# A fused transformer block: where the first block's scores, values and gate are worked out, by which engine and in which step

## The chip, the cores and the metric

The kernel runs on one core of one Trainium2 chip. Its metric is the time of one execution on the device in microseconds. The kernel before was timed three times: 1420.10, 1420.78 and 1422.68 us, median 1420.78 us. One further execution was recorded by the hardware profiler; it took 1421.69 us, and all rows below are from it.

The engines are named as the profile names them: TensorE (PE; PEld is its weight load), VectorE (DVE), ScalarE (ACT), GpSimd (POOL) and SyncE (SP).

## What is computed

A token row of 512 positions, with 16 meta tokens ahead of it (528 keys), passes a forgetting-attention mixer, a SwiGLU, a gated linear recurrence and a second feed-forward network. The change lies in the first of these alone:

```python
def fox_mixer(h, w_in, b_f, q_gain, k_gain, w_out):
    proj = h @ w_in
    q, k, v, gate, f_logit = jnp.split(proj, [D, 2 * D, 3 * D, 4 * D], axis=-1)
    q = rms_norm(q.reshape(B, L, FOX_HEADS, FOX_HEAD_DIM), q_gain)
    k = rms_norm(k.reshape(B, L, FOX_HEADS, FOX_HEAD_DIM), k_gain)
    log_f = jax.nn.log_sigmoid(f_logit + b_f)
    c = jnp.cumsum(log_f, axis=1).transpose(0, 2, 1)
    ...
    s = jnp.einsum('bhqd,bhkd->bhqk', q_blk, k) * (FOX_HEAD_DIM ** -0.5)
    s = s + (c_q[..., :, None] - c_k[..., None, :])
    s = jnp.where(pos_k[None, :] <= pos_q[:, None], s, -jnp.inf)
    p = jax.nn.softmax(s, axis=-1)
    o = jnp.einsum('bhqk,bhkd->bhqd', p, v)
    ...
    o = o * jax.nn.sigmoid(gate)
    return o @ w_out
```

There are 16 heads of 64 channels (D is 1024) and four blocks of 128 queries; block i sees 16 + 128 (i + 1) keys, so 144, 272, 400 and 528.

## The kernel before, in words

**Tiling and staging.** Two heads make a pair that fills 128 partitions; there are eight pairs, t = 0 to 7. For each pair the four projections q, k, v and gate are made one after the other. Products are taken in a high and a low part of each operand, which makes three matmuls for each of the eight 128-row tiles of the contraction. q and gate have one PSUM tile of 512 columns, k and v two of 264. ScalarE writes the high part of the next weights (L170), VectorE the low part (L180).

**The order of the work.** The loop at the end of `fox` advances a `Weave` once per eighth of a projection: one step is three matmuls of 512 columns or six of 264, and a pair has 32 steps (q is steps 0 to 7, k 8 to 15, v 16 to 23, gate 24 to 31). What else a pair needs is entered in the weave with `at(delay, fn)`, so that it is issued between the matmuls of a later step; every engine then runs its instructions in the order in which they were issued. The delays stand in one row of constants (`F_V` to `F_0`), with special tuples for the first pairs (`K_0`, `Q_1`). A step called 10' below is step 10 of the pair whose projections are being made; the attention work in it is that of the pair before.

**What is woven in.** `head_norm` takes a finished q or k out of PSUM (L392), squares it on ScalarE (L394) and, as high and low part, on GpSimd (L396, L397), sums the squares per head on TensorE into a tile `tp` (L323), and forms the inverse root by L222, L225 and L226 on ScalarE and L224, L229 and L230 on VectorE; L406 scales q or k by it. `got_g` takes the gate out, forms a log-sigmoid (L467, L468 and L472 on ScalarE, L473 and L474 on GpSimd) and its exponential (L477).

`attend` has eight units u = 2 i + s for query block i and head s. `scores` makes the logits in PSUM (L502 the mask, L504 and L506 the products), the row maximum (L510, L512) and the exponential with its row sum (L515). For u = 6 and 7 the 528 keys do not fit one tile and make two pieces of 264. Two steps later `scaled` multiplies the probabilities by the inverse sum (L521, L523). Eight steps after its scores, `flip` transposes the unit on TensorE (L535) into one or two tiles and copies them out: L537 on ScalarE or L539 on VectorE, as the table `F_E` says for each unit. `values` multiplies the flipped probabilities of both heads with v into the tile `plog` (L547), and `gated` multiplies that with the gate (L553).

**PSUM tiles.** `mm` has three tiles, which q, the two of k, the two of v and the gate take in turn; so the second tile of v is the first of k, and has to be read out by L392 before v's matmuls may write it. `tp` has two: the sums, the flips, the flip of v (L422) and the second score pieces all take them in turn. `py` has two, for the scores; `plog` has one.

**Steps.** For the pairs t = 2 to 7, u0 to u4 are scored at the end of the pair's own steps and in 0' to 5', u6 at 7', u7 at 9', flips at two-step distance up to 17', values at 9', 13', 17' and 21', `gated` at 23'. The sums of q are issued at 10', those of k at 18'.

Of the kernel before, what the change touches and what calls it, by code (L numbers as in the profile page):

```python
# [20 lines left out]
F32 = mybir.dt.float32  # L21
# [4 lines left out]
AF = mybir.ActivationFunctionType  # L26
OP = mybir.AluOpType
# [3 lines left out]
P = 128  # L31
D = 1024
KT = D // P
T = 512
# [35 lines left out]

A_W, A_Q, A_K, A_R = 1, 1, 2, 5

F_E = 1, 1, 1, 1, 1, 0, 0, 0


F_V, Q_U, Q_R, Q_H, Q_L, K_U, K_R, K_H, K_L, F_S, F_F, F_O, F_G, F_N, F_0 = 6, 3, 2, 12, 1, 2, 2, 6, 2, 12, 8, 4, 12, 2, 5

K_0, Q_1 = (7, 2, 10, 2), (5, 2, 12, 1)


class Weave:
# [5 lines left out]
    def at(self, delay, fn, *args):  # L87
        self.todo.setdefault(self.step + delay, []).append((fn, args))
# [11 lines left out]
class Net:  # L100
# [147 lines left out]
    def fox(self):  # L248
        nc, tc, a = self.nc, self.tc, self.a
# [8 lines left out]
        pp = self.pp  # L258

        def mm():  # L260
            return pp.tile([P, T], F32, name="mm", bufs=3)
# [23 lines left out]
        NB = T // P  # L285
# [62 lines left out]
        def f_bank():  # L348
            return pp.tile([P, T], F32, name="py", bufs=2)
# [34 lines left out]
        at = w.at  # L384
# [28 lines left out]
        def got_v(t, pv):  # L413
            v1 = wk.tile([P, TM], F32, name="v1", bufs=1)
            for p, o, n in pv:
                nc.vector.tensor_mul(v1[:, o:o + n], p, r1[:, o:o + n])

            def flip():
                vt = vts[t % 2]
                tp = pp.tile([P, T], F32, name="tp", bufs=2)  # L420
                for j in range(NB):
                    nc.tensor.transpose(tp[:, j * P:(j + 1) * P], v1[:, j * P:(j + 1) * P], self.ident)  # L422
                nc.scalar.activation(vt[:, 0:NB].rearrange("p j d -> p (j d)"), tp, AF.Copy)
                tp = pp.tile([P, T], F32, name="tp", bufs=2)
                nc.tensor.transpose(tp[:NM, :P], v1[:, T:TM], self.ident)
                nc.vector.tensor_copy(vt[:NM, NB], tp[:NM, :P])

            at(F_V, flip)

        def got_q(t, pq):  # L430

# [28 lines left out]
        def got_g(t, pg):  # L460
            sg = wk.tile([P, T], F32, name="sg", bufs=2)
            nc.vector.tensor_mul(sg, pg[0][0], r1[:, NM:])


            def exponential():
                e = sgs[t, 1] = wk.tile([P, T], F32, name="se", bufs=1)
                nc.scalar.activation(e, sg, AF.Abs)  # L467
                nc.scalar.activation(e, e, AF.Exp, scale=-1.0)  # L468

            def logarithm():  # L470
                e = sgs[t, 1]
                nc.scalar.activation(e, e, AF.Ln, bias=1.0)  # L472
                nc.gpsimd.tensor_scalar(sg, sg, 0.0, None, op0=OP.min)  # L473
                nc.gpsimd.tensor_sub(sg, sg, e)  # L474

            def sigmoid():
                nc.scalar.activation(sg, sg, AF.Exp)  # L477

            at(F_G, exponential)
            at(F_G + 2, logarithm)  # L480
            at(F_G + 6, sigmoid)
            sgs[t] = sg
# [3 lines left out]
        def attend(t):  # L486
            vt = vts[t % 2]
            pts, po = [], []

            def scores(i, s):  # L490
                kw = NM + P * (i + 1)
                qi = slice(i * P, (i + 1) * P)
                ps = pp.tile([P, T], F32, name="py", bufs=2)
                if kw > T:
                    n = kw // 2
                    pieces = [(ps, 0, n), (pp.tile([P, T], F32, name="tp", bufs=2), n, n)]
                else:
                    pieces = [(ps, 0, kw)]
                for p, o, n in pieces:
                    m0 = max(o, kw - P)  # L500
                    if m0 < o + n:
                        nc.tensor.matmul(p[:, m0 - o:n], self.identb, self.maskb, start=True, stop=False,  # L502
                                         skip_group_check=True)
                    nc.tensor.matmul(p[:, :n], qs[:, s, qi], kd[:, s, o:o + n], start=(m0 >= o + n), stop=False,  # L504
                                     skip_group_check=True)
                    nc.tensor.matmul(p[:, :n], q2[:, s, qi], k2[:, s, o:o + n], start=False, stop=True,  # L506
                                     skip_group_check=True)
                mx = wk.tile([P, 6], F32, name="mx", bufs=4)
                for e, (p, o, n) in enumerate(pieces):
                    nc.vector.tensor_reduce(mx[:, e:e + 1], p[:, :n], axis=AX.X, op=OP.max, negate=True)  # L510
                if len(pieces) > 1:
                    nc.vector.tensor_tensor(mx[:, 0:1], mx[:, 0:1], mx[:, 1:2], op=OP.min)  # L512
                for e, (p, o, n) in enumerate(pieces):
                    c = pt_off[i] + o
                    nc.scalar.activation(pb[s][:, c:c + n], p[:, :n], AF.Exp, bias=mx[:, 0:1],  # L515
                                         accum_out=mx[:, 2 + e:3 + e])

                def scaled():
                    if len(pieces) > 1:
                        nc.vector.tensor_add(mx[:, 2:3], mx[:, 2:3], mx[:, 3:4])  # L520
                    nc.vector.reciprocal(mx[:, 4:5], mx[:, 2:3])  # L521
                    pbi = pb[s][:, pt_off[i]:pt_off[i] + kw]
                    nc.vector.tensor_scalar(pbi, pbi, mx[:, 4:5], None, op0=OP.mult)  # L523

                at(F_N, scaled)

            def flip(i, s):
                if i == 0:
                    pts.append(wk.tile([P, PW], F32, name=f"pt{s}", bufs=1))
                for j0 in range(0, i + 2, 4):  # L530
                    n = min(4, i + 2 - j0) * P
                    c = pt_off[i] + j0 * P
                    tp = pp.tile([P, T], F32, name="tp", bufs=2)
                    for o in range(0, n, P):
                        nc.tensor.transpose(tp[:, o:o + P], pb[s][:, c + o:c + o + P], self.ident)  # L535
                    if F_E[2 * i + s]:
                        nc.scalar.activation(pts[s][:, c:c + n], tp[:, :n], AF.Copy)  # L537
                    else:
                        nc.vector.tensor_copy(pts[s][:, c:c + n], tp[:, :n])  # L539

            def values(i):
                if i == 0:
                    po.append(pp.tile([P, T], F32, name="plog", bufs=1))
                for j in range(i + 2):
                    c = pt_off[i] + j * P
                    for s in range(2):
                        nc.tensor.matmul(po[0][s * HD:(s + 1) * HD, i * P:(i + 1) * P],  # L547
                                         vt[:, j, s * HD:(s + 1) * HD], pts[s][:, c:c + P],
                                         start=(j == 0), stop=(j == i + 1), skip_group_check=True)

            def gated():
                sg = sgs[t]
                nc.vector.tensor_mul(sg, po[0], sg)  # L553
                nc.scalar.activation(ogh[:, t], sg, AF.Copy)

            def gated_lo():
                sg = sgs.pop(t)
                nc.vector.tensor_sub(ogl[:, t], sg, ogh[:, t].bitcast(F32))

            s0 = F_S + (0 if t else F_0)  # L560
            for u in range(2 * NB):
                at(s0 + 2 * u, scores, u // 2, u % 2)
                at(s0 + F_F + 2 * u, flip, u // 2, u % 2)
            for i in range(NB):
                at(s0 + F_F + F_O + 4 * i + 2, values, i)
            at(s0 + F_F + F_O + 4 * NB, gated)
            at(s0 + F_F + F_O + 4 * NB + 2, gated_lo)

        kinds = ((got_q, False), (got_k, True), (got_v, True), (got_g, False))
        forget_1()  # L570
        got_q(0, q0)
# [15 lines left out]
        for n in range(self.EARLY):  # L587
            p = mm() if n < 3 else f_bank()
# [16 lines left out]
        for m in range(KT):  # L605
            if m < self.EARLY:
                p = early[m]
            else:
                p = mm()
# [1037 lines left out]
```

## Time and profile before

| | |
|---|---|
| median of three runs | 1420.78 us |
| profiled execution | 1421.69 us |
| its span | 1419.9 us |
| TensorE busy | 1349.7 us, 95% |
| VectorE busy | 741.5 us, 52% |
| ScalarE busy | 535.6 us, 38% |
| GpSimd busy | 143.9 us, 10% |

The span reaches from the first to the last instruction; 1.79 us of the execution lie outside it. The first block's attention lies between about 40 and 340 us of the span, and repeats every 37 us. Shares of busy time are means over the whole kernel, most of which the change does not touch, so the rows below are from the attention alone. [...]

### The profile page before, as it was taken

The numbers are of one execution on the slowest core, as the hardware profiler recorded it, in microseconds if no ns is written. First come the engines' busy times: TensorE is split into PE (matmuls) and PEld (weight loads), VectorE is DVE, ScalarE is ACT, GpSimd is POOL, SyncE is SP. The second block draws the span as 40 slices with busy tenths as digits, with TensorE's granted clock in tenths as the row PEclk, the third lists the DMA queues.
The fourth block names the chain that finished last, engine by engine and source line by source line (L and its number), as shares of the span: only waits on it lengthen the run. The fifth ranks groups of instructions, "written<-read, shape, count | busy, mean of one in ns | idle before, by whom it ended". The sixth has DMA issues, their size and how long they took to land.

```text
span 1419.9 us, 20806 instructions
## 1 busy us (share of the span) xinstructions
PE 1349.7 (95%) x8506; PEld 1027.8 (72%) x8506; DVE 741.5 (52%) x1321; ACT 535.6 (38%) x988; POOL 143.9 (10%) x127
## 2 busy tenths in 40 slices
PE   7899999999999999999999999999999999988895
PEld 6788888888788888888887888875656656545452
DVE  7887788784654433444455666533342342332234
ACT  6766666664523222323443354522111111111114
POOL 2312222211200000000322121000000000000001
PEclk9999999999999999999999999999999999999998
DMA  4111111113332322223221222698999999999994
GB/s 161 69 44 61 60 61 60 60 60 119 116 111 90 109 99 89 89 94 113 90 89 60 89 90 81 263 400 322 404 421 419 420 420 421 420 419 421 420 421 195
DMA packets 41346, 282.26 MB, mean 199 GB/s; under 512 B 4736, under 2 KB 4992, under 8 KB 7840
## 3 DMA queue, kind: packets, MB, share of 16 engines
q1 hardware_dynamic: 40464, 280.05, 49.6%
q8 instruction: 68, 1.11, 0.3%
q10 hardware_dynamic: 784, 0.85, 0.2%
q14 instruction: 30, 0.25, 0.1%
HBM read 278.72 MB, written 2.10 MB: 198 GB/s over the span
## 4 chain that ended last, share of the span: by engine, by line
PE 70%; DMA 13%; DVE 9%; ACT 4%; issue 1%; POOL 1%; SPq 0%; ACTq 0%; DVEq 0%; POOLq 0%
PE mm L207 20%; PE mm L336 8%; PE py L207 8%; PE tp L207 8%; DMA wring<-in_w_dram 7%; PE tp L1269 5%; PE plog L1322 4%; DMA v<-in_w_dram 3%; DMA wraw<-in_w_dram 3%; PE py L1301 3%; PE mm L792 2%; PE tp L1280 1%; DVE pb L523 1%; PE mm L1287 1%; PE plog L547 1%
## 5 line engine op out<-in xcount | busy, mean ns | idle before, releaser
L180 DVE TENSOR_TENSOR whl<-wraw,whl 128x1024 fp32r<-128x1024 f32 x138 | 181.5, 1315 | 102.4 <-ACT whl L170 102.1
L336 PE MATMUL mm<-xh,whl 128*128 128x264 f32 (+1 forms) x736 | 183.5, 333 | 3.8 <-DVE q L392 2.8
L170 ACT ACTIVATE whl<-wraw 128x1024 fp32r<-128x1024 f32 x138 | 144.5, 1050 | 109.6 <-PE mm L207 45.9
L207 PE MATMUL mm<-xh,whl 128*128 128x512 f32 x544 | 176.1, 397 | 0.0
L336 PEld LDWEIGHTS mm<-xh,whl 128*128 128x128 f32 x736 | 120.8, 191 | 18.8 <-issue 3.4
L1269 PEld LDWEIGHTS tp<-h,xt 128*128 128x128 f32 x992 | 114.2, 194 | 19.1 <-PE plog L1322 7.5
L1269 PE MATMUL tp<-h,xt 128*128 128x128 f32 x992 | 120.1, 280 | 0.0
L207 PEld LDWEIGHTS mm<-xh,whl 128*128 128x128 f32 x544 | 102.3, 188 | 23.0 <-issue 2.3
L207 PE MATMUL mm<-xl,whl 128*128 128x512 f32 x272 | 106.2, 390 | 0.0
L1282 DVE COPY sv<-tp 128x3 f32<-128x3 f32 x16 | 2.6, 160 | 188.2 <-PE tp L1280 188.2
L336 PE MATMUL mm<-xl,whl 128*128 128x264 f32 (+1 forms) x368 | 100.0, 325 | 0.0
L1272 ACT ACTIVATE h<-tp,vecs 128x128 f32<-128x128 f32 x124 | 35.3, 368 | 158.1 <-PE tp L1269 158.1
L1322 PE MATMUL plog<-wring,h 128*32 128x512 f32 x624 | 72.8, 596 | 8.6 <-ACT h L1272 4.6
L1289 DVE TENSOR_TENSOR acc<-acc,mm 128x512 f32<-128x512 f32 (+1 forms) x120 | 73.2, 673 | 6.0 <-PE mm L1288 6.0
L207 PE MATMUL mm<-ogh,whl 128*128 128x512 f32 x224 | 73.8, 396 | 0.0
L635 POOL TENSOR_TENSOR ss<-ss,sq 128x512 f32<-128x512 f32 x21 | 29.1, 1401 | 371.1 <-ACT sq L631 349.1
L207 PE MATMUL py<-xh,whl 128*128 128x512 f32 x208 | 65.9, 392 | 0.0
L207 PE MATMUL tp<-xh,whl 128*128 128x512 f32 x208 | 65.2, 390 | 0.0
L336 PEld LDWEIGHTS mm<-xl,whl 128*128 128x128 f32 x368 | 62.2, 191 | 3.0
L207 PEld LDWEIGHTS mm<-xl,whl 128*128 128x128 f32 x272 | 51.2, 188 | 11.5 <-issue 1.4
L1287 PE MATMUL mm<-h,ss 128*128 128x512 f32 (+1 forms) x128 | 56.5, 442 | 2.2 <-DVE acc L1289 0.5
L1451 POOL TENSOR_TENSOR wring<-acc,wring 128x512 f32<-128x512 f32 x4 | 5.0, 1282 | 494.6 <-DVE acc L1289 494.6
(438 smaller groups left out, 2508.5 us busy)
## 6 DMA issues: line engine op xcount, KB each, us to landing
wring<-in_w_dram SPq DMA_DIRECT2D x124, 1024.0 KB, 19.8
wraw<-in_wd_dram SPq DMA_DIRECT2D x69, 1024.0 KB, 4.7
whl<-in_w_dram SPq DMA_DIRECT2D x27, 1024.0 KB, 19.8
v<-in_w_dram SPq DMA_DIRECT2D x20, 1024.0 KB, 19.8
wraw<-in_w_dram SPq DMA_DIRECT2D x18, 1024.0 KB, 19.8
h<-in_xT_dram SPq DMA_DIRECT2D x8, 256.0 KB, 6.1
acc<-in_w_dram SPq DMA_DIRECT2D x2, 1024.0 KB
out_dram<-wring SPq DMA_DIRECT2D x4, 512.0 KB, 4.7
```

The lines of the kernel that those rows point to most:

```text
L170: self.nc.scalar.activation(hl[:, 0], raw, AF.Copy)
L180: self.nc.vector.tensor_sub(hl[:, 1], raw, hl[:, 0].bitcast(F32))
L207: self.nc.tensor.matmul(out, w, x[:, first + k], start=(at + k == 0 and e == 0), stop=(at + k == of - 1 and e == 2))
L336: nc.tensor.matmul(p[:rows, :m], w[:, wi, k], xx[:, k, o:o + m], start=(n == 0), stop=(n == 3 * KT - 1))
L635: nc.gpsimd.tensor_add(ss, ss, sq)
L792: nc.tensor.matmul(pv[b], x[:, k, bs], w2[:, wi, k % 2], start=(k == 0 and e == 0), stop=(k == KT - 1 and e == 2))
L1269: nc.tensor.matmul(p[:, k], self.xt[:, b, (k0 + k) * P:(k0 + k + 1) * P], oh[:, 1, b], start=(b + k == 0), stop=(b == NB - 1), skip_group_ ...
L1272: nc.scalar.activation(xs[:, k0 + k], p[:, k], AF.Copy, scale=self.vec(V_FN2, k0 + k))
L1287: nc.tensor.matmul(pc, gt[:, b * P:(b + 1) * P], yh[:, hs], start=True, stop=False)
L1289: nc.vector.tensor_add(acc[b][:, hs], acc[b][:, hs] if q else self.xt[:, b, hs], pc)
L1301: nc.tensor.matmul(py[js, o:o + c], hT[:, e, js], w, start=(e == 0), stop=(e == 1), skip_group_check=True)
L1322: nc.tensor.matmul(ps[32 * j:32 * j + 32], xs[:, k, 32 * j:32 * j + 32], self.ring[q, k][:, j * T:(j + 1) * T], start=(k == 0), stop=(k == ...
```

## The change

The second score piece of u = 6 and 7 goes to the tile `plog` and no longer to `tp`, its exponential is issued ahead of that of the first piece, and u7 is scored and flipped one step later (10' and 18'). The values are taken four steps later (`F_O` 8 for 4), so at 13', 17', 21' and 25', and `gated` at 27'. The multiplication by the inverse sum goes from VectorE to ScalarE. The two GpSimd steps of the gate become one VectorE instruction. The flip of u7 is copied out by ScalarE (the last entry of `F_E`), the sums of k are issued a step later (`K_U`, 3 for 2), those of q for pair 1 two steps earlier (`Q_1`), and the flip of v of pair 0 three steps later (`V_0`).

```diff
-F_E = 1, 1, 1, 1, 1, 0, 0, 0
+F_E = 1, 1, 1, 1, 1, 0, 0, 1
...
-F_V, Q_U, Q_R, Q_H, Q_L, K_U, K_R, K_H, K_L, F_S, F_F, F_O, F_G, F_N, F_0 = 6, 3, 2, 12, 1, 2, 2, 6, 2, 12, 8, 4, 12, 2, 5
+F_V, Q_U, Q_R, Q_H, Q_L, K_U, K_R, K_H, K_L, F_S, F_F, F_O, F_G, F_N, F_0 = 6, 3, 2, 12, 1, 3, 2, 6, 2, 12, 8, 8, 12, 2, 5
-K_0, Q_1 = (7, 2, 10, 2), (5, 2, 12, 1)
+K_0, Q_1, V_0 = (7, 2, 10, 2), (3, 2, 14, 1), 9
...
-            at(F_V, flip)
+            at(F_V if t else V_0, flip)
...
-                nc.gpsimd.tensor_scalar(sg, sg, 0.0, None, op0=OP.min)
-                nc.gpsimd.tensor_sub(sg, sg, e)
+                nc.vector.scalar_tensor_tensor(sg, sg, 0.0, e, op0=OP.min, op1=OP.subtract)
...
-                    pieces = [(ps, 0, n), (pp.tile([P, T], F32, name="tp", bufs=2), n, n)]
+                    pieces = [(ps, 0, n), (pp.tile([P, T], F32, name="plog", bufs=1), n, n)]
...
-                for e, (p, o, n) in enumerate(pieces):
+                for e, (p, o, n) in reversed(list(enumerate(pieces))):
...
-                    nc.vector.tensor_scalar(pbi, pbi, mx[:, 4:5], None, op0=OP.mult)
+                    nc.scalar.activation(pbi, pbi, AF.Copy, scale=mx[:, 4:5])
...
             for u in range(2 * NB):
-                at(s0 + 2 * u, scores, u // 2, u % 2)
-                at(s0 + F_F + 2 * u, flip, u // 2, u % 2)
+                last = int(u + 1 == 2 * NB)
+                at(s0 + 2 * u + last, scores, u // 2, u % 2)
+                at(s0 + F_F + 2 * u + last, flip, u // 2, u % 2)
```

The line numbers of the changed kernel are those of the kernel before up to L472; in it the new VectorE instruction is L473, the exponential of the gate L476, and the multiplication, now on ScalarE, keeps L523.

**ScalarE, pair in the steady state, from u6's exponentials to the inverse root of q.** Before (`pb_128` and `pb_129` hold the probabilities of the two heads, `pt_` the flipped ones, `rr` is the root's tile):

```order
L515 ACTIVATE pb_128,mx<-py,mx 128x264
L515 ACTIVATE pb_128,mx<-tp,mx 128x264
L170 ACTIVATE whl<-wraw 128x1024
L537 ACTIVATE pt_2253<-tp 128x384
L515 ACTIVATE pb_129,mx<-py,mx 128x264
L515 ACTIVATE pb_129,mx<-tp,mx 128x264
L222 ACTIVATE rr<-tp,epsc 128x512
```

And in the changed kernel:

```order
L515 ACTIVATE pb_128,mx<-plog,mx 128x264
L515 ACTIVATE pb_128,mx<-py,mx 128x264
L523 ACTIVATE pb_129<-pb_129,mx 128x400
L170 ACTIVATE whl<-wraw 128x1024
L537 ACTIVATE pt_2249<-tp 128x384
L523 ACTIVATE pb_128<-pb_128,mx 128x528
L515 ACTIVATE pb_129,mx<-plog,mx 128x264
L515 ACTIVATE pb_129,mx<-py,mx 128x264
L222 ACTIVATE rr<-tp,epsc 128x512
L225 ACTIVATE rr<-rr 128x512
```

Two multiplications (L523) now stand between u6's exponentials and the root L222, which still follows u7's exponentials; of the two pieces the one in `plog` now comes first.

**VectorE, from the root of q to the flips of u6.** Before (`q_2273` is q, `q_2420` the k of the same pair):

```order
L229 TENSOR_TENSOR rs_t<-rs_t,rs_x 128x512
L230 SCALAR_TENSOR_TENSOR rr<-rs_t,rr 128x512
L406 SCALAR_TENSOR_TENSOR q_2273<-q_2273,qg,rr 128x512
L539 COPY pt_2253<-tp 128x512
L392 TENSOR_TENSOR q_2420<-mm,r_119 128x264 x2
L539 COPY pt_2233<-tp 128x512
L539 COPY pt_2233<-tp 128x128
L180 TENSOR_TENSOR whl<-wraw,whl 128x1024
L539 COPY pt_2253<-tp 128x512
```

And in the changed kernel, where q is `q_2269` and k `q_2409`:

```order
L229 TENSOR_TENSOR rs_t<-rs_t,rs_x 128x512
L230 SCALAR_TENSOR_TENSOR rr<-rs_t,rr 128x512
L406 SCALAR_TENSOR_TENSOR q_2269<-q_2269,qg,rr 128x512
L539 COPY pt_2249<-tp 128x512
L473 SCALAR_TENSOR_TENSOR sg<-sg,se 128x512
L392 TENSOR_TENSOR q_2409<-mm,r_119 128x264 x2
L539 COPY pt_2229<-tp 128x512
L539 COPY pt_2229<-tp 128x128
L180 TENSOR_TENSOR whl<-wraw,whl 128x1024
```

The gate's instruction L473 now stands ahead of the read-out of k (L392), and the two copies of u7's flip are gone.

**TensorE, around the flip of u7.** The difference, with + and - for the changed kernel against the kernel before (`pt_1399` and `pt_1419` are the flipped probabilities, `vt_138` is v):

```order
+L336 MATMUL mm<-xl,whl 128x264 x2
+L336 MATMUL mm<-xh,whl 128x264 x2
 L535 MATMUL tp<-ident,pb_129 128x128 x5
-L547 MATMUL plog<-pt_1399,vt_138 64x128
-L547 MATMUL plog<-pt_1419,vt_138 64x128
-L547 MATMUL plog<-pt_1399,vt_138 64x128
-L547 MATMUL plog<-pt_1419,vt_138 64x128
-L547 MATMUL plog<-pt_1399,vt_138 64x128
-L547 MATMUL plog<-pt_1419,vt_138 64x128
-L547 MATMUL plog<-pt_1399,vt_138 64x128
-L547 MATMUL plog<-pt_1419,vt_138 64x128
 L323 MATMUL tp<-sqh,hones 128x264
```

The flip of u7 stands one step later than before, and the third block's values, which stood between it and the sums of k (L323), have moved behind these sums.

## Rows read from the trace of the kernel before

**Rows 1.** The page of the kernel before: its first line, and of part 1 the line with each engine's busy time, share of the span and instructions.

```profile
span 1419.9 us, 20806 instructions
...
PE 1349.7 (95%) x8506; PEld 1027.8 (72%) x8506; DVE 741.5 (52%) x1321; ACT 535.6 (38%) x988; POOL 143.9 (10%) x127
```

**Rows 2.** The busy time of each engine in two stretches of the trace, with the granted TensorE clock: one whole period of the steady state, and what follows the longest wait of the start.

```profile
158.00:195.00 37.00, 36.11 (x269) 31.06 (x269) 29.70 (x62) 24.93 (x53) 8.60 (x6) 1.00 0.16 58
...
64.50:67.90 3.40, 3.40 (x18) 3.12 (x17) 3.33 (x5) 3.12 (x8) 2.10 (x2) 0.52 0.00 0
```

**Rows 3.** What TensorE waited for between 0 and 500 us: engine, tile and line that waited, what released it, us in total, how often, longest.

```profile
PE tp L535 <- ACT pb L515: 2.3, 6, 0.4
...
PE tp L323 <- DVE pt L539: 1.9, 6, 0.3
...
PE mm L336 <- DVE q L392: 2.8, 1, 2.8
```

**Rows 4.** TensorE's timeline over one period of the steady state: start us, us from the first start to the last end, line, operation, tiles, shape, count, and in brackets idle time before it with its releaser. L547 has two records for each of its matmuls.

```profile
172.30 0.28 PE L506 MATMUL py<-k,q 128*128 128x264 f32 x1
...
172.66 0.22 PE L502 MATMUL tp<-maskb,identb 128*128 128x128 bf16 x1
...
173.10 0.66 PE L547 MATMUL plog<-pt,vt 128*64 128x128 f32 x8
...
175.47 0.40 PE L336 MATMUL mm<-xh,whl 128*128 128x264 f32 x2
...
176.25 0.65 PE L535 MATMUL tp<-ident,pb 128*128 128x128 f32 x4 [0.38 <-ACT pb L515]
...
178.21 0.60 PE L535 MATMUL tp<-ident,pb 128*128 128x128 f32 x4
...
178.75 0.88 PE L547 MATMUL plog<-pt,vt 128*64 128x128 f32 x12
...
181.12 0.71 PE L535 MATMUL tp<-ident,pb 128*128 128x128 f32 x5
...
181.58 0.49 PE L336 MATMUL mm<-xh,whl 128*128 128x264 f32 x2
...
181.91 0.41 PE L336 MATMUL mm<-xl,whl 128*128 128x264 f32 x2
...
182.15 0.66 PE L336 MATMUL mm<-xh,whl 128*128 128x264 f32 x4
...
183.77 1.09 PE L547 MATMUL plog<-pt,vt 128*64 128x128 f32 x16
...
185.19 0.36 PE L323 MATMUL tp<-sqh,hones 128*128 128x264 f32 x1 [0.33 <-DVE pt L539]
...
185.67 0.39 PE L323 MATMUL tp<-sql,hones 128*128 128x264 f32 x1
...
194.75 0.23 PE L502 MATMUL py<-maskb,identb 128*128 128x128 bf16 x1
```

**Rows 5.** VectorE's timeline in the same period.

```profile
171.58 1.48 DVE L523 TENSOR_SCALAR pb<-pb,mx 128x400 f32<-128x400 f32 x1
...
176.81 0.69 DVE L224 TENSOR_SCALAR rs_x<-tp 128x512 f32<-128x512 f32 x1 [0.94 <-ACT rr L222]
...
178.21 0.69 DVE L229 TENSOR_TENSOR rs_t<-rs_t,rs_x 128x512 f32<-128x512 f32 x1
...
179.74 0.90 DVE L406 SCALAR_TENSOR_TENSOR q<-q,qg,rr 128x512 f32<-128x512 f32 x1
...
180.56 0.68 DVE L539 COPY pt<-tp 128x512 f32<-128x512 f32 x1
...
181.19 0.77 DVE L392 TENSOR_TENSOR q<-mm,r 128x264 f32<-128x264 f32 x2
```

**Rows 6.** ScalarE's timeline in the same period.

```profile
171.57 0.48 ACT L515 ACTIVATE pb<-py,mx 128x264 f32<-128x264 f32 x1 [0.19 <-DVE mx L521]
...
175.16 0.48 ACT L515 ACTIVATE pb<-py,mx 128x264 f32<-128x264 f32 x1 [1.23 <-DVE mx L520]
...
176.09 0.69 ACT L222 ACTIVATE rr<-tp,epsc 128x512 f32<-128x512 f32 x1
...
179.80 0.63 ACT L472 ACTIVATE se<-se 128x512 f32<-128x512 f32 x1
```

**Rows 7.** Groups of instructions between 30 and 440 us, different shapes apart: line, engine, operation, tiles, shape, count, then us in total and mean ns of one, then the idle time ahead of them.

```profile
L523 DVE TENSOR_SCALAR pb<-pb,mx 128x528 f32<-128x528 f32 x16 | 7.9, 496 | 0.6
...
L394 ACT ACTIVATE sq<-q 128x528 f32<-128x528 f32 x8 | 5.2, 647 | 14.1 <-DVE q L392 14.1
...
L230 DVE SCALAR_TENSOR_TENSOR rr<-rs_t,rr 128x512 f32<-128x512 f32 x8 | 5.5, 692 | 0.3
...
L537 ACT ACTIVATE pt<-tp 128x512 f32<-128x512 f32 x8 | 4.7, 582 | 0.9 <-PE tp L535 0.9
```

**Rows 8.** The timeline of the start, in order VectorE, GpSimd (two) and TensorE.

```profile
61.91 1.55 DVE L406 SCALAR_TENSOR_TENSOR q<-q,qg,rr 128x512 f32<-128x512 f32 x1
...
53.30 2.30 POOL L397 TENSOR_TENSOR sql<-sq,sqh 128x512 fp32r<-128x512 f32 x1
...
61.56 1.35 POOL L474 TENSOR_TENSOR sg<-sg,se 128x512 f32<-128x512 f32 x1 [2.50 <-ACT se L472]
...
63.86 0.39 PE L336 MATMUL mm<-xh,whl 128*128 128x264 f32 x1 [2.85 <-DVE q L392]
```

## The prediction

> **What bounds the kernel now.** I read the page's first part, then the table of stretches, the waits of TensorE, and last the timelines of three engines side by side over one period. The page shows TensorE busy for 95% of the span [rows 1]. That is a mean over the whole kernel, and the change touches the attention alone. There the stretch of one period shows 36.11 us of 37.00 busy at the full clock, 2.4 GHz; no other engine is above 29.70 [rows 2]. So TensorE's matmuls set the pace, and a pair can gain no more than the time in which they stand still.
>
> The waits by line come to little: 2.3 us in six places where a flip waits for an exponential, and 1.9 us in six where the sums of k wait for a copy [rows 3]. Both recur once a pair. Read from start to start, the timeline shows more, since a matmul of 264 columns is followed by the next 0.12 us later (two of them from 181.91 to 182.15). I count four holes in a pair [rows 4]: 0.25 us ahead of u7's second piece (172.30 and one pitch to 172.66), 0.53 ahead of u4's flip (175.47 and two pitches to 176.25), 0.40 ahead of the sums of k at 185.19, and 0.36 between their first two matmuls. Together 1.54 us. The first two are waits for one of the two `tp` tiles while a score piece sits in it. The next pair's first scores at 194.75 end the stretch that I walk.
>
> **The change, part by part.** I walk one period on the clock of these rows, giving each engine the order of the changed kernel and the durations of before.
>
> *Tile.* With the second pieces in `plog`, both waits for `tp` go: -0.25 and -0.53 for TensorE. `plog` is free there, since the values come later.
>
> *Values four steps later.* Nothing is added; 8 records for 0.50 us leave the place ahead of u4's flip [rows 4], and each later group moves behind the flip that it stood before. So TensorE comes to the flip of u5 at 178.21 - 0.25 - 0.53 - 0.50 = 176.93. The work is late rather than gone: it had covered waits, and the places that it leaves are the ones to watch.
>
> *Multiplication on ScalarE.* VectorE loses the two long ones, 496 ns for 528 columns and, for 400 columns beside GpSimd, 1.48 us [rows 5, 7]. ScalarE's price is not in the trace. The nearest row is its square of 528 columns, 647 ns [rows 7]; below, a 264-column exponential starts 0.48 us wide [rows 6]. Back to back the pitch is some 0.1 shorter than the duration, so I take 0.50 for 400 and 0.55 for 528 columns, bounds 0.4 to 0.9. From u6's exponentials at 171.57 ScalarE now has two exponentials 0.93, the multiplication 0.50, the weights' high part 0.94, a flip's copy 0.40, the multiplication 0.55 and two exponentials 0.93, so it comes to L222 at 175.82, against 176.09 [rows 6]. Before, it had 1.23 us of idle time there, ahead of u7's exponentials; the multiplications fill it. VectorE becomes freer, and the root of q is only 0.27 us earlier.
>
> *What hangs on the root.* VectorE's L224 follows L222 by 0.72 (176.09 to 176.81) and takes 0.69 [rows 5, 6], so it releases the tile of the sums at about 177.4. The flip of u5 takes this tile and stands ready at 176.93: a wait of 0.5 that before did not exist. L406 comes at 179.47 and the copy of u5's flip (L539) at 180.29, both 0.27 ahead of their rows. The fifth transpose of u6's flip needs the tile of that copy; TensorE is there at 180.2 and waits until 180.95, 0.7.
>
> *Gate on VectorE.* Two GpSimd steps become one VectorE instruction: 692 ns by the nearest one of its form [rows 7], bounds 0.4 to 0.9. It is ahead of L392 in the order and waits for L472, which ScalarE reaches at 179.80 - 0.27 + 0.55 (u7's multiplication) = 180.08 and ends at 180.71. So it runs from 180.85, and L392, behind it, at 181.55 for 181.19 [rows 5, 6]. Queued behind both are k's square, its sums, and the second tile of v, which TensorE may not write until L392 has read the first half of k: at 182.0, where the row at 181.58 shows v's matmuls going on without a stop [rows 4]. TensorE is there at 181.2: 0.8 us.
>
> *Flip of u7 on ScalarE, sums of k a step later.* Before, 1.09 us of values stood between this flip and the sums (183.77), and still the two holes of 0.40 and 0.36 were left [rows 4]. Now the sums follow the flip at once and need its tiles, copied out by ScalarE in 582 ns for the first 512 columns [rows 7] and some 0.3 for the rest: 0.9 us, for 0.76. The values that had stood there follow later, where there is nothing to cover.
>
> So a pair has 0.5 + 0.7 + 0.8 + 0.9 = 2.9 us of holes for 1.54: +1.3, and the next pair's first scores come at 196.1 instead of 194.75. Chain and deadline of k's scaling move too, but end at 195.4, ahead of that. Bounds: with the multiplication at 0.4 and the gate at 0.4 every chain is some 0.3 earlier, which takes 0.6 off the sum; at 0.9 each it adds 0.6. That is +0.7 to +1.9 a pair. Pairs 2 to 7 make six periods: +7.8, from +4.2 to +11.4.
>
> *Start.* L406 of pair 1 took 1.55 us beside L474 on GpSimd, 0.90 in the steady state; with GpSimd's step gone L392 is 0.65 earlier, and so the wait that ends at 63.86 [rows 5, 8]. After that wait the granted clock was 0.52 for 3.4 us, near the 1.2 GHz level [rows 2]. With a shorter wait this may stay away: -1.65, half of 3.4. The earlier sums of pair 1 have to wait for `sql`, which ends at 55.60, +1.1 [rows 8]. The flip of v of pair 0, moved later, gains nothing, because the scores behind it wait for the root of k. Together -1.2, bounds -3 and +1. At the end of the attention `gated` is eight steps ahead of the end, which hides it: 0.
>
> **GpSimd and VectorE beside each other.** L406's 1.55 us lasted until GpSimd's L474 ended at 62.91; the multiplication at 171.58 took 1.48 for an unhindered 0.4 to 0.5, beside L397 on GpSimd [rows 5, 8]. The Trainium skill, "SBUF — State Buffer", section "Who interferes with whom", states that a VectorE instruction with two SBUF inputs, or in a two-port mode, and a GpSimd instruction that reads SBUF shut each other out for the whole instruction. The rows agree. By it the change should free VectorE of about 1 us a pair. But the weights' low part L180 now stands where the multiplication stood, with two SBUF inputs, and would be the one to wait. By the skill that leaves 0.15 us a pair either way, 0.9 in all; I leave it out of the sum.
>
> **The sum.** The profiled execution is 1421.69 us, its span 1419.9 and 1.79 around it; 1421.69 + 7.8 - 1.2 = 1428.3. It is 0.91 above the median of the three runs, so against that I forecast 1427.4, put down as 1427.
>
> **Rivals.** *The gate does not hold L392 up (chance 0.20).* If ScalarE reaches L472 0.4 us earlier, or the second tile of v is not waited for, the 0.8 goes: +0.5 a pair, +3.0 - 1.2 = 1422.6 by the median. For it: the margin is 0.35 us. Against: L473 is ahead of L392 in the order, and L472 has gained a multiplication ahead of it.
>
> *No new hole but that of u6's flip (0.22).* If the copies on ScalarE and the release by L392 come in time, only the chain through L222 counts, which is 0.27 earlier. TensorE resumes u6's flip at 180.95; before, that fifth transpose ran at about 181.4. Behind it the two old holes of 0.76 are gone and the 0.88 of the second block's values (178.75 [rows 4]) is added: 0.45 + 0.76 - 0.88, so -0.33 a pair, -2.0 and with the start -3.2: 1417.6. For it: ScalarE has 12 us free in a period [rows 2]. Against: those 12 us do not lie between u6's exponentials and L222.
>
> *The clock falls (0.06), slower still.* In the start a wait of 2.85 was followed by the 1.2 GHz level [rows 2, 8]. Should a pair's new waits, 2 us within 4, do the same, a further 1.7 a pair comes: 1427.4 + 10.2 = 1437.6. Against: after the holes of the steady state, up to 0.53 us, the clock stays at 2.4 GHz [rows 2].
>
> *ScalarE binds as walked (0.52)*, with its own range of 1422 to 1432: the six pairs from +4.2 to +11.4, the start's bounds within.
>
> **Chances and range.** No change means within 0.2%, about 2.8 us, which is what a measurement of this kernel can tell. Below 1418 lies most of the second rival: faster 0.22. Within 2.8 us lie the first rival and the edge of the others: same 0.20. The rest is slower, 0.58, by the walk and the clock. The range 1417 to 1432 takes in the first two rivals' values and the walk, and leaves out the clock and the tails.
>
> **What would show it.** Right, step by step: no wait of a flip for an exponential; ScalarE with no idle time ahead of u7's exponentials, and L222 within 0.4 us of its old place in the period; L392 right behind L473; a wait of v's matmuls for L392 in each pair; waits of the sums of k for ScalarE's copy; a period of 38.3. Wrong: a period under 37.0, or L392 with no L473 next to it in time, or L222 more than 0.6 us earlier.

## The result and the profile after

The changed kernel takes 1429.26 us (median of four, 1428.58 to 1429.94), the kernel before 1420.44 us in the runs that are compared with it: a ratio of 1.0062, with a 95% interval of 1.005 to 1.0075. It is slower by 8.8 us, and lies 2.3 us above the forecast of 1427, inside its range.

The first lines of the changed kernel's page stand beside [rows 1]:

```profile
span 1427.6 us, 20801 instructions
...
PE 1351.8 (95%) x8506; PEld 1024.6 (72%) x8506; DVE 711.9 (50%) x1249; ACT 569.1 (40%) x1068; POOL 127.1 (9%) x111
```

VectorE has lost 29.6 us of work, ScalarE gained 33.5, GpSimd lost 16.8, and TensorE does the same matmuls in a span 7.7 us longer. TensorE's waits up to 500 us show what came in place of [rows 3] (engine, tile and line; releaser; us in total, times, longest):

```profile
PE tp L323 <- ACT pt L537: 4.2, 7, 0.7
...
PE mm L336 <- DVE q L392: 4.2, 7, 1.2
...
PE tp L535 <- DVE rs_x L224: 3.8, 7, 1.7
...
PE tp L535 <- DVE pt L539: 1.2, 6, 0.2
```

The wait of a flip for an exponential, 2.3 us before, is gone. Four others recur once a pair: u5's flip for L224, u6's fifth transpose for the copy of u5's flip, v for L392, and the sums of k for ScalarE's copy of u7's flip. To see what they cost, take the same period as in [rows 4 to 6]. A hole is read from start to start there, less the pitch at which such matmuls follow each other; the idle time in brackets is shorter, because a record ends after the next one has begun (185.01 and 0.39, then 185.24). The period now begins with the read-out of q at 172.78 and ends with the next one at 211.15, so it lasts 38.37 us against 37.00. A time of before plus 3.13 (172.78 less 169.65, where that read-out lay before) is its place here. VectorE:

```profile
172.78 0.69 DVE L392 TENSOR_TENSOR q<-mm,r 128x512 f32<-128x512 f32 x1 [0.74 <-PE mm L336]
...
174.60 1.20 DVE L180 TENSOR_TENSOR whl<-wraw,whl 128x1024 fp32r<-128x1024 f32 x1
...
175.76 1.22 DVE L520 TENSOR_TENSOR mx<-mx 128x1 f32<-128x1 f32 x1
...
177.88 0.16 DVE L512 TENSOR_TENSOR mx<-mx 128x1 f32<-128x1 f32 x1
...
179.78 0.69 DVE L224 TENSOR_SCALAR rs_x<-tp 128x512 f32<-128x512 f32 x1 [1.74 <-ACT rr L222]
...
182.64 0.75 DVE L406 SCALAR_TENSOR_TENSOR q<-q,qg,rr 128x512 f32<-128x512 f32 x1
...
183.31 0.68 DVE L539 COPY pt<-tp 128x512 f32<-128x512 f32 x1
...
183.93 0.69 DVE L473 SCALAR_TENSOR_TENSOR sg<-sg,se 128x512 f32<-128x512 f32 x1
...
184.53 0.77 DVE L392 TENSOR_TENSOR q<-mm,r 128x264 f32<-128x264 f32 x2
...
211.15 0.69 DVE L392 TENSOR_TENSOR q<-mm,r 128x512 f32<-128x512 f32 x1 [0.74 <-PE mm L336]
```

ScalarE and GpSimd in the same period:

```profile
175.63 0.62 ACT L523 ACTIVATE pb<-pb,mx 128x400 f32<-128x400 f32 x1
...
176.15 1.05 ACT L170 ACTIVATE whl<-wraw 128x1024 fp32r<-128x1024 f32 x1
...
177.47 0.73 ACT L523 ACTIVATE pb<-pb,mx 128x528 f32<-128x528 f32 x1
...
178.13 0.48 ACT L515 ACTIVATE pb<-plog,mx 128x264 f32<-128x264 f32 x1
...
179.06 0.69 ACT L222 ACTIVATE rr<-tp,epsc 128x512 f32<-128x512 f32 x1
...
183.28 0.61 ACT L472 ACTIVATE se<-se 128x512 f32<-128x512 f32 x1
```

```profile
174.67 2.30 POOL L397 TENSOR_TENSOR sql<-sq,sqh 128x512 fp32r<-128x512 f32 x1
```

TensorE:

```profile
176.66 0.40 PE L323 MATMUL tp<-sqh,hones 128*128 128x512 f32 x1
...
177.02 0.50 PE L323 MATMUL tp<-sql,hones 128*128 128x512 f32 x1
...
179.76 0.41 PE L336 MATMUL mm<-xh,whl 128*128 128x264 f32 x2
...
180.53 0.66 PE L535 MATMUL tp<-ident,pb 128*128 128x128 f32 x4 [0.36 <-DVE rs_x L224]
...
183.26 0.60 PE L535 MATMUL tp<-ident,pb 128*128 128x128 f32 x4
...
184.05 0.33 PE L535 MATMUL tp<-ident,pb 128*128 128x128 f32 x1 [0.19 <-DVE pt L539]
...
184.14 0.37 PE L336 MATMUL mm<-xh,whl 128*128 128x264 f32 x1
...
185.01 0.39 PE L336 MATMUL mm<-xh,whl 128*128 128x264 f32 x1 [0.51 <-DVE q L392]
...
188.19 0.71 PE L535 MATMUL tp<-ident,pb 128*128 128x128 f32 x5
...
189.57 0.36 PE L323 MATMUL tp<-sqh,hones 128*128 128x264 f32 x1 [0.67 <-ACT pt L537]
...
199.25 0.23 PE L502 MATMUL py<-maskb,identb 128*128 128x128 bf16 x1
```

Read the three engines together. ScalarE has nothing idle in front of any of its rows from 175.63 to L222 at 179.06, which is 175.93 on the clock of before: 0.16 earlier than in [rows 6], although VectorE has been freed (25.96 us busy in a period of 38.37, and ScalarE 29.09). L224 follows, and u5's flip waits for it at 180.53. On VectorE L406, the copy L539, the gate's L473 and L392 come without a gap, and L473 begins just as L472 ends on ScalarE (183.28 + 0.61 = 183.89). TensorE waits for L392 at 185.01. The last hole is ahead of 189.57, where the sums of k wait for ScalarE.

### The profile page after: what moved, and what is told of

Same layout as the page of the kernel before. It is cut to its first block, busy times and chain, and to the rows that moved or that the text cites. A ratio compares the mean times of both kernels' runs of the same rounds, so it can differ in the third digit from the quotient of the medians.

```text
span 1427.6 us, 20801 instructions
## 1 busy us (share of the span) xinstructions
PE 1351.8 (95%) x8506; PEld 1024.6 (72%) x8506; DVE 711.9 (50%) x1249; ACT 569.1 (40%) x1068; POOL 127.1 (9%) x111
## 4 chain that ended last, share of the span: by engine, by line
PE 75%; DMA 10%; ACT 6%; DVE 6%; issue 2%; POOL 0%; ACTq 0%; SPq 0%; DVEq 0%; POOLq 0%
PE mm L207 19%; PE mm L336 9%; PE py L207 8%; PE tp L207 8%; PE tp L1270 6%; DMA wring<-in_w_dram 6%; PE plog L1323 5%; DMA v<-in_w_dram 3%; PE py L1302 3%; PE mm L793 2%; PE plog L547 2%; PE tp L1281 1%; DMA wraw<-in_w_dram 1%; PE mm L1288 1%; ACT pb L515 1%
## 5 line engine op out<-in xcount | busy, mean ns | idle before, releaser
L180 DVE TENSOR_TENSOR whl<-wraw,whl 128x1024 fp32r<-128x1024 f32 x138 | 180.6, 1308 | 109.0 <-ACT whl L170 108.7
L336 PE MATMUL mm<-xh,whl 128*128 128x264 f32 (+1 forms) x736 | 188.6, 335 | 5.4 <-DVE q L392 4.2
L1323 PEld LDWEIGHTS plog<-wring,h 128*32 128x32 f32 x624 | 18.1, 109 | 50.3 <-issue 40.4
```

What stands on the lines that cost most here:

```text
L180: self.nc.vector.tensor_sub(hl[:, 1], raw, hl[:, 0].bitcast(F32))
L336: nc.tensor.matmul(p[:rows, :m], w[:, wi, k], xx[:, k, o:o + m], start=(n == 0), stop=(n == 3 * KT - 1))
L1323: nc.tensor.matmul(ps[32 * j:32 * j + 32], xs[:, k, 32 * j:32 * j + 32], self.ring[q, k][:, j * T:(j + 1) * T], start=(k == 0), stop=(k == ...
```

## The experiments

The theory: two chains, one through ScalarE to the root of q and one through L472 and the gate's instruction to L392, meet TensorE, whose matmuls for the values no longer stand ahead of them. One rival puts the loss on the values alone (whatever is earlier waits at the next hole), one on the multiplications on ScalarE, one on the tile. The period is the mean distance of the starts of q's read-outs (L392, 512 columns) from pair 3 to pair 7; "start" is the time from the read-out of pair 1 to that of pair 2, which holds the start's waits. From 100 to 360 us the granted clock is 1.00 in every trace, so the periods compare; in the start it is not, and the times differ by that too (see "Start" below).

| kernel | start, us | period, us | median, us | ratio to before, 95% interval |
|---|---|---|---|---|
| before | 44.24 | 37.00 | 1420.44 | 1 |
| changed | 45.84 | 38.37 | 1429.26 | 1.005 to 1.0075 |
| gate_late | 44.44 | 37.78 | 1422.39 | 1.000 to 1.0019 |
| u6_late | 44.10 | 38.46 | 1429.83 | 1.0043 to 1.0076 |
| both_late | 41.18 | 37.22 | 1419.07 | 0.9981 to 1.000 |
| mul_dve | 44.61 | 39.39 | 1434.97 | 1.0082 to 1.0116 |
| gate_pool | 44.80 | 37.90 | 1426.28 | 1.0022 to 1.0051 |
| flip7_dve | 43.17 | 38.48 | 1429.45 | 1.0047 to 1.0086 |
| after_fill_2 | 44.49 | 38.15 | 1427.29 | 1.0032 to 1.0084 |
| fill | 41.27 | 36.98 | 1418.11 | 0.9972 to 0.9992 |
| fill_lo | 41.27 | 36.29 | 1413.00 | 0.9929 to 0.9963 |
| tile_only | 46.65 | 39.05 | 1436.38 | 1.0101 to 1.0135 |

**gate_late.**

```diff
+            def minus():
+                e = sgs[t, 1]
                 nc.vector.scalar_tensor_tensor(sg, sg, 0.0, e, op0=OP.min, op1=OP.subtract)
...
             at(F_G + 2, logarithm)
+            at(F_G + 4, minus)
```

> The changed kernel, with the gate's VectorE instruction issued two steps later, so that it stands behind the read-out of k (L392) and not ahead of it. Theory (the chain: in a period of 38.37 us TensorE waits 0.51 for L392 because the gate's instruction is ahead of it): L392 comes 0.6 us earlier, the 0.51 goes and nothing takes its place, the period is 37.9 and the time about 3 us below the changed kernel, near 1426. Rival (the cover: the values moved away leave gaps, and whatever is made earlier only waits at the next one): the sums of k wait as much longer, the period stays within 0.1 of 38.4 and the time near 1429.

The period fell by 0.59 to 37.78: the wait for L392 is gone and the other waits have not grown, so the rival "whatever is earlier waits at the next hole" falls for this one. The time fell by 6.9 us where 3 were expected. The pairs give 6 x 0.59 = 3.5, the start 1.4, and 1.3 lies ahead of pair 1's read-out of q (48.89 for 50.20), which this edit doesn't explain: that time differs from kernel to kernel by up to 3.2 us (48.41 in both_late, 51.58 in flip7_dve).

**u6_late.**

```diff
-                at(F_N, scaled)
+                at(4 if len(pieces) > 1 and s == 0 else F_N, scaled)
```

> The changed kernel, with the multiplication of u6 alone (528 columns on ScalarE) two steps later, behind the root of q and no longer ahead of it. Theory (the chain, two members of it): the root L222 comes 0.6 us earlier in the period and the waits of the flip of u5 (0.36) and of u6's fifth transpose (0.19) go; but L392 stays where it is, since the gate's instruction ahead of it still waits for ScalarE's L472, so the wait for L392 grows from 0.51 to about 1.0 and the period stays within 0.1 of 38.4, the time near 1429. Rival (the multiplications on ScalarE ahead of the root are the whole cost): the period falls by 0.5 to 37.8 and the time by 3 us to 1426.

As the theory said: the root came earlier, the waits for L224 and for the copy of u5's flip are gone from the steady state, and the period is no shorter (38.46). Over one period the wait for L392 has taken it all, 1.1 us for 0.51, because the gate's instruction ahead of it now waits for ScalarE (TensorE's wait, then VectorE's row):

```profile
PE mm L336 <- DVE q L392: 1.1, 1, 1.1
...
182.95 0.69 DVE L473 SCALAR_TENSOR_TENSOR sg<-sg,se 128x512 f32<-128x512 f32 x1 [0.56 <-ACT se L472]
```

**both_late** is both edits.

> The changed kernel with both edits, the gate's instruction behind L392 and the multiplication of u6 behind the root of q. Theory (the chain): now all three waits go, 0.36 + 0.19 + 0.51, more than the sum of what each edit gives alone; the period is 37.3 to 37.4 and the time about 6 us below the changed kernel, near 1423. Rival (each edit has its own price, independent of the other): the period falls by what the two edits gave alone, added up. Rival (the cover): 38.2 or more, time 1428 or more.

The period is 37.22, and 1.15 is more than the two edits gave alone (0.59 and -0.09), so they do not have prices of their own: the later multiplication of u6 is worth nothing alone and 0.56 once the gate's instruction is out of the way. VectorE goes from the copy of u5's flip (here L543) to L392 at once, and the gate's instruction (here L476) follows behind the next copies:

```profile
173.98 0.68 DVE L543 COPY pt<-tp 128x512 f32<-128x512 f32 x1
...
174.58 0.76 DVE L392 TENSOR_TENSOR q<-mm,r 128x264 f32<-128x264 f32 x2
...
176.05 0.99 DVE L476 SCALAR_TENSOR_TENSOR sg<-sg,se 128x512 f32<-128x512 f32 x1
```

Six periods account for 6.9 us, the start for 4.7, of which more below, and the time ahead of pair 1's read-out for 1.8; 0.7 of this is lost again at the end of the attention and 1.5 behind it. The profiled execution is 11.3 us shorter (1418.05 for 1429.35), the median 10.2.

**mul_dve** puts `tensor_scalar` on VectorE back in the place of the ScalarE multiplication.

> The changed kernel with the multiplication by the inverse sum back on VectorE for all units. Theory (the chain): no help. The multiplication of u5 waits again for GpSimd's sql and delays u7's row maximum, so u7's exponentials and the root come within 0.3 us of where they are; the gate's instruction is behind the flip's copy in any case. The period is 38.2 to 38.6 and the time within 2 us of the changed kernel's. Rival (ScalarE's multiplications are what the change pays for): the root is 0.6 us earlier or more, the period 37.8 or less, the time 1426 or less.

Neither came: 39.39 is 1.0 us a pair worse. Three rows of VectorE and two of ScalarE show the place:

```profile
177.77 1.21 DVE L180 TENSOR_TENSOR whl<-wraw,whl 128x1024 fp32r<-128x1024 f32 x1
...
179.29 0.50 DVE L523 TENSOR_SCALAR pb<-pb,mx 128x528 f32<-128x528 f32 x1
...
179.70 0.42 DVE L510 TENSOR_REDUCE mx<-py 128x1 f32<-128x264 f32 x1
```

```profile
178.25 0.48 ACT L537 ACTIVATE pt<-tp 128x384 f32<-128x384 f32 x1
...
180.75 0.48 ACT L515 ACTIVATE pb<-plog,mx 128x264 f32<-128x264 f32 x1 [2.02 <-DVE mx L512]
```

With u7 scored one step later, the multiplication of u6 comes ahead of u7's row maximum on VectorE (179.29 before 179.70), and ScalarE stands idle for 2.02 us ahead of u7's exponentials. I had counted the multiplication of u5 and the weights but not that of u6. With u7 one step later, the multiplication on ScalarE is therefore worth 1.0 a pair; it is not what the change pays for.

**gate_pool** puts the two GpSimd steps back in the place of the VectorE instruction.

> The changed kernel with the gate's two steps back on GpSimd. Theory (the chain): L392 again follows the flip's copy at once, 0.6 us earlier, so the wait of 0.51 goes; GpSimd's later sqh and sql end before the sums of k ask for them. Period 37.8 to 38.1, time 1425 to 1427.5. Rival (GpSimd's two steps and VectorE lock each other out, so L406 or sql come so much later that nothing is gained): period 38.3 or more, time 1429 or more.

37.90, within the theory's numbers. L392 follows the copy at once, and its wait is gone:

```profile
182.41 0.68 DVE L540 COPY pt<-tp 128x512 f32<-128x512 f32 x1
...
183.01 0.76 DVE L392 TENSOR_TENSOR q<-mm,r 128x264 f32<-128x264 f32 x2
```

**tile_only** is the kernel before with the tile, the later u7, the later values and the later sums of k alone.

> The kernel before with the score pieces in the tile of the values, u7 one step later, the values four steps later and the sums of k one step later; the multiplication stays on VectorE, the gate on GpSimd, u7's flip on VectorE. Theory (the tile's 0.78 a pair is paid back by the values' lost cover, and u7's row maximum comes later, behind u6's multiplication on VectorE): a wait of the flip of u5 for L224 of over 1 us, period 38.4 to 39.0, the time 1429 to 1433, so the tile part alone makes the kernel slower. Rival (the tile part is a gain, and the other parts bring the loss): the period is 36.2 to 36.6 and the time 1416 to 1418.

39.05 and 1436.38, a little beyond what the theory gave: the tile edit by itself, with what it needs, is slower than the whole change. Its waits up to 360 us:

```profile
PE tp L535 <- DVE rs_x L224: 12.1, 7, 2.7
...
PE tp L323 <- DVE pt L539: 4.6, 6, 0.8
...
PE tp L535 <- DVE pt L539: 3.1, 7, 0.7
```

Three of the changed kernel's four places, with larger waits: 1.6 us a pair for L224 (12.1 less the longest, over six) where the changed kernel has 0.36. L392 is not among them, with the gate on GpSimd. The root is as late as in mul_dve, L222 7.25 us behind the read-out of q in both (6.28 in the changed kernel), and for the same reason: u6's multiplication on VectorE (178.60) is ahead of u7's row maximum (179.02). The rival that the tile is a gain and the other parts the loss has fallen for these four parts together; which of them costs how much was not tried apart.

**flip7_dve** sets the last entry of `F_E` back to 0.

> The changed kernel with the flip of u7 copied out by VectorE again. Theory (the hole ahead of the sums of k is there because nothing stands in it, and either engine copies at once): VectorE is free at that point and takes 0.88 for the two copies where ScalarE takes 0.77, so the hole is 0.0 to 0.15 longer, the period 38.4 to 38.5, the time within 1.5 us of the changed kernel's. Rival (ScalarE's copy is what the sums of k wait for, as one of the costs of the change): the hole falls back from 1.05 to 0.76, the period 38.1, the time 1427.5.

38.48 and no change of the time that can be measured: which engine copies u7's flip matters by no more than 0.11 us a pair.

**after_fill** and **after_fill_2** are one kernel:

```diff
-                at(s0 + F_F + F_O + 4 * i + 2, values, i)
+                at(s0 + F_F + F_O + (2, 6, 7, 14)[i], values, i)
```

> The changed kernel with only the values of the third block at step 18'. Theory (each hole belongs to its own place): the hole ahead of the sums of k (1.05 from start to start) is filled, the three others stay at 0.36, 0.19 and 0.51; 0.5 to 0.6 of it is gained, then the scores meet L448. Period 37.8 from 38.37, time about 3 us below the changed kernel, near 1426. Rival (the chain through the root is all that counts): period within 0.1 of 38.4, 1429.

> The same kernel as in the run after_fill (the changed kernel with the values of the third block at step 18'), whose profiled execution cannot be read. Theory and rival as there: period 37.8 with the hole ahead of the sums of k filled, the other three holes in place and a new wait of the scores for L448, against 38.4 with nothing gained; by the times that run gave (1427.65) the period is about 38.1.

The medians of the two agree (1427.65 and 1427.29); the rows are from the second. The period is 38.15, a gain of 0.22 where 0.5 to 0.6 was expected. The hole is filled and the others stand (0.36, 0.18, 0.51). On TensorE's rows from the flip of u7 to the next pair's scores:

```profile
187.12 0.71 PE L535 MATMUL tp<-ident,pb 128*128 128x128 f32 x5
...
188.78 0.39 PE L323 MATMUL tp<-sqh,hones 128*128 128x264 f32 x1
...
197.92 0.33 PE L504 MATMUL py<-kd,qs 128*128 128x144 f32 x1 [0.43 <-ACT kd L448]
```

From the flip to the sums it takes 1.66 us (187.12 to 188.78) where it took 1.38 with the hole: the values are a little longer than the hole was. So the sums, and k's scaling behind them, come 0.28 later after the flip, and of the 0.6 of slack ahead of the scores (L448 ends at 198.64 in the changed kernel, L504 starts at 199.28) half is used up before TensorE has gained anything.

**fill** is the same edit on top of both_late.

> The kernel with both edits before, and the values of the third block moved to step 18', where they stand on TensorE between the flip of u7 and the sums of k (as they did before the change) and not after the sums. Theory (the cover: the hole of 1.0 us ahead of the sums of k exists because nothing stands there, and 1.0 us of values fit into it): the hole shrinks to 0.2 or less. But then the next pair's scores meet the end of k's scaling on ScalarE (L448), which leaves only 0.6 of slack, so that about 0.5 of the 1.0 comes back as a wait of the scores for L448; the period goes from 37.2 to 36.6 or 36.7 and the time from 1419 to about 1416. Rival (the sums of k wait for something else, the copies come later as well): the hole stays and the period is 37.1 or more.

36.98, where 36.6 or 36.7 was expected: the hole is gone and 0.24 is gained, with 0.43 to 0.45 us of waiting for L448 in five pairs and 0.79 in the first, for the reason just given.

**fill_lo** issues the low parts of q one step later as well (`Q_L`, 2 for 1).

> The same, and the low parts of q (L439, L440) one step later, so that on VectorE they stand behind the scaling of k (L229, L230, L406) and not ahead of it. Theory: k's scaling ends 1.9 us earlier, the wait of the scores for L448 goes, and the whole 1.0 is gained; the period is 36.2 to 36.3, the time about 1413 to 1414. Rival (TensorE is not held by k's scaling): no difference from the run without this edit, within 0.1 us a pair.

As expected: 36.29 a pair and 1413.00 us. In a whole period TensorE has no wait left (columns as in [rows 2]: busy time of TensorE, its weight load, VectorE, ScalarE, GpSimd, then the granted clock):

```profile
163.58:199.86 36.28, 36.27 (x269) 30.81 (x268) 26.06 (x52) 29.26 (x63) 6.05 (x4) 1.00 0.17 59
```

It is 0.54% faster than the kernel before (ratio 0.9946, interval 0.9929 to 0.9963), and 16 us faster than the changed kernel, 12.5 of them in six periods, with the same instructions on the same engines.

## Why the prediction was right, and where it was not

*The tile.* Right: the two waits for `tp` are gone.

*Values four steps later.* Right that the places they leave are the ones to watch. The hole ahead of the sums of k is where the third block's values had stood, and fill_lo shows that with these matmuls back in it and the chains out of the other three holes a pair takes 36.29. That the other three holes come from the values too is argued and not shown: no run puts the first and second block's values back.

*Multiplication on ScalarE.* The two prices, start to start, came out at 0.52 us for 400 columns (175.63 to 176.15) and 0.66 for 528 (177.47 to 178.13), for 0.50 and 0.55. L222 was put at 175.82 on the clock of before and came at 175.93. My reason, that ScalarE has no idle time left, holds.

*What hangs on the root.* From start to start u5's flip has a hole of 0.53 (179.76 and two pitches of 0.12 to 180.53), for 0.5 predicted. L406 and L539 came at 179.51 and 180.18 on the clock of before, for 179.47 and 180.29. The fifth transpose waits 0.43 by the same reading (183.26 and four pitches of 0.09 to 184.05), 0.19 by the profile's, for 0.7: the one term that came out clearly smaller. The walk had TensorE at this transpose at 180.2 on the clock of before; it came at 180.49 (183.62), since the flip itself began at 180.13 and its first four transposes take 0.36.

*Gate on VectorE.* Right: 0.69 us long; L392 at 181.40 for 181.55; a hole of 0.75 (184.14 and one pitch to 185.01) for 0.8. That an earlier root alone would only lengthen this wait was not said, and u6_late and both_late show it.

*Sums of k.* A hole of 0.93 (188.19 and five pitches to 189.57) for 0.9. Of the two reasons given only one counts: the missing values (after_fill and fill close the hole), and not that ScalarE copies (flip7_dve).

So a pair has 0.53 + 0.43 + 0.75 + 0.93 = 2.64 us of holes, and 0.13 more ahead of the second sum of q at 177.02, for 2.9 predicted. Less the 1.54 of before that is +1.23 of the +1.37 measured; the remaining 0.14 was not traced to a place. The period is 38.37 for 38.3, and the next scores come at 196.12 on the clock of before (199.25) for 196.1. Six pairs gave +8.2 us for +7.8.

*Start.* This term was wrong, in sign too: -1.2 was forecast, and up to pair 2's read-out of q it is 96.04 for 95.65, +0.4 us. That it missed by no more is luck, since 1.2 us were gained ahead of pair 1's read-out (50.20 for 51.41), for which no term was given, and 1.6 lost behind it. Of the waits that I named, v's for L392 fell by 1.70, to 1.15 us, where 0.65 was forecast; the sums of pair 1 wait 0.84 for `sql`, for 1.1; and the flip of v of pair 0 gains nothing, as forecast, its wait of 1.29 being one of the scores for L448 of 1.28 now. The step that failed is that the lower clock would stay away, put at -1.65. Behind the shorter wait for L392 it did stay away (1.00 from 60 to 68 us), but it fell later and for longer, with a wait of 1.66 us for L224 that the prediction didn't list (TensorE's row, then stretches with the columns of [rows 2]):

```profile
69.45 1.11 PE L535 MATMUL tp<-ident,pb 128*128 128x128 f32 x4 [1.66 <-DVE rs_x L224]
...
68.00:72.00 4.00, 2.54 (x12) 2.55 (x13) 2.31 (x6) 3.94 (x11) 0.00 (x0) 0.57 0.23 96
...
72.00:76.00 4.00, 4.00 (x24) 3.34 (x24) 2.75 (x5) 3.87 (x7) 0.00 (x0) 0.57 0.01 2
```

That is the 1.2 GHz level for most of both stretches, and TensorE was busy for only 2.54 of the first 4 us. At 0.57 of the full clock these 8 us lose some 3.4 (an estimate, 8 times 0.43), where the kernel before lost 1.7 (0.57 from 64 to 68): +1.7 for the -1.65. But the waits alone do not decide it. flip7_dve has the same ones in its start (1.16 for L392, 1.66 for L224) and stays at 2.4 GHz (1.00 from 72 to 76 us as well):

```profile
70.82 0.66 PE L535 MATMUL tp<-ident,pb 128*128 128x128 f32 x4 [1.66 <-DVE rs_x L224]
...
68.00:72.00 4.00, 2.34 (x18) 2.13 (x19) 1.34 (x6) 3.94 (x11) 0.00 (x0) 1.00 0.56 233
```

By the same count after_fill_2, again with these waits, lost 1.7; u6_late, with 1.04 for L224, lost 1.7 too; both_late, with 1.07 and no wait for L392, lost nothing. So of the 4.7 us by which both_late's start is shorter 3.4 go with the clock by this estimate, and that its edits brought them isn't shown. What makes the clock fall stays open, and as each kernel has one trace, so does whether it falls alike in all executions of one kernel.

*Elsewhere.* At the first read-out behind the attention (L611 before, L612 now) the changed kernel is 8.8 us late: 0.4 + 8.2 and 0.2 at the end of the attention, where 0 was forecast. By the end of the span 7.7 are left. In the other runs the stretch behind the attention differs from that of before by -1.2 to +0.4 us, so I take nothing from the -1.1 here; its cause was not looked for.

*The rivals.* The gate does hold L392 up, the holes other than u6's do exist, and the clock, though it fell in the start, stayed at 2.4 GHz in the steady state (granted 1.00 from 100 to 360 us). By its own bounds the walk's range should have reached 1433 (+11.4 for the pairs, +1 for the start), not 1432.

*VectorE and GpSimd.* By the rule of the Trainium skill ("SBUF — State Buffer", section "Who interferes with whom") L180 and L397 would shut each other out. The trace agrees: L180 began first (174.60), L397 lasts 2.30 instead of the 1.30 us of before and ends at 176.97, and the second sum of q starts 0.13 late. The prediction had L180 as the one to wait, and put either order at 0.15 us a pair. One row that the prediction took for this was misread: L406 of pair 1 did not end with L474 at 62.91 but 0.55 later, at 63.46 (61.91 and 1.55).

## What to carry to other kernels

Taking a wait away gains nothing if the work that had covered other waits leaves its place at the same time: before moving matmuls to a later step, list what is waited for at the place that they leave. Where two chains end close together at the bound engine, try them together as well as apart, since one of them alone can show nothing (u6_late) and the two more than their sum (both_late). An engine with a quarter of its time free can still bind, as ScalarE does here: what counts is whether it is free in the few microseconds between the wait's cause and its end. And compare such edits by the period: in the start the granted clock differs by some 3.4 us of work between kernels with the same waits there (the changed kernel and flip7_dve).

## What had not been expected

An addition of one column on VectorE (L520 at 175.76, two operands in SBUF) took 1.22 us, where it took 0.15 in the kernel before. It ends with GpSimd's L397 (176.97), and u7's row maximum stands behind it. In the kernel before (times there 3.13 earlier) L397 was over when the addition came:

```profile
171.53 1.30 POOL L397 TENSOR_TENSOR sql<-sq,sqh 128x512 fp32r<-128x512 f32 x1
...
174.98 0.15 DVE L520 TENSOR_TENSOR mx<-mx 128x1 f32<-128x1 f32 x1
```

By itself it costs the changed kernel next to nothing. u7's row maximum is complete when L512 ends at 178.04, and ScalarE, held by u6's multiplication, begins u7's exponentials at 178.13. By these rows either of the two alone keeps the root within about 0.1 us of where it is. In u6_late and both_late both stand behind u7's row maximum, and in u6_late L222 comes 0.54 us earlier in the period.
